# A hybrid decoder layer: moving activations at a stride of 1088 bytes, and row tiles that take turns in the down projection

## The chip, the cores and the metric

The kernel runs on one core of one Trainium2 chip. The metric is the device time of one execution in microseconds (us); the median of three runs stands for a kernel. The engines are named as in the profile: PE is TensorE (PEld its weight loads), DVE is VectorE, ACT is ScalarE, POOL is GpSimd, SP issues most of the DMAs.

## The reference

One decoder layer over 272 tokens (16 meta tokens and 256 of the sequence), model dimension 2048, all in float32:

```
u = rmsnorm(h);  proj = u @ w_in                       # 2048 x 7176
8 retention heads and 4 mLSTM heads -> mix (2048 features)
h = h + mix @ w_out                                    # 2048 x 2048, the output projection
u = rmsnorm(h);  up = causal_dwconv(u @ w_up)          # 2048 x 11264, the up projection
gate, val = split(up);  h = h + (silu(gate) * val) @ w_down   # 5632 x 2048, the down projection
return rmsnorm(h)[:, 16:]
```

## The kernel before

**Matrix products.** A weight is read once from HBM in pieces of 512 KB (`load_w`, lines 123 to 132), and split into two parts: ScalarE rounds it to float32r (`whi`, line 129) and VectorE takes the rest (`wlo`, line 131). The activations are split in the same way (`xh`/`xl`, `mixh`/`mixl`, `uh`/`ul`, `mh`/`ml`). A product is three matmuls per pair of tiles: high by high, high weight by low activation, low weight by high activation.

**Input, output and up projections** keep the activations feature-major: a tile `[128, 16, columns]` holds 16 feature tiles in a row of each partition. The weight (128 x 128) is the stationary operand, and one feature tile of the activations, all tokens, is the moving one. A piece of 512 KB is a half output tile: 8 feature tiles, so 24 matmuls (`mmk`, lines 134 to 141: eight pairs of lines 138 and 139, then eight of line 141). The moving columns are 272 tokens (`T`) in the input projections, or 258 (`NQ`, tokens 14 on) or 262 where the earliest tokens are not needed. `xh` and `xl` (lines 180 and 181) have 272 columns, so one feature tile lies 1088 bytes behind the last; a 258-column matmul on them reads from column 14. `mixh` and `mixl` (lines 175 and 176, 32 half tiles of the output projection at line 526) and `uh` and `ul` (lines 499 and 500, 176 half tiles of the up projection at line 595) have 258 columns, a stride of 1032 bytes.

**The down projection** (lines 587 to 648) turns the operands round. It runs twice, for each half of the 5632 features, after the up projection of that half. The weights are the moving operand, 512 columns; the stationary one is 128 tokens of `mh` or `ml`. A half has 4 blocks of 512 output columns (loop over `b`), a block has 11 steps (`q`), and a step has one 512 KB piece with two feature tiles. For each step `product` is called for row tile 0 (tokens 0 to 127), six matmuls into one PSUM bank, and then for row tile 1, six into another. In the last block of all row tile 1 runs 4 steps behind, so that row tile 0 is normed and stored meanwhile. `done` (line 620) adds a finished block to the residual; `finish` (line 571) does the last norm and the store.

**Order.** A scheduler of the framework orders the instructions by estimated times. All 512 KB pieces go through one DMA queue (SP) into 4 buffers (`wraw`); there are 5 buffers of `whi` and 5 of `wlo`. Output tiles of the projections rotate through 4 PSUM banks (`mmps`), blocks of the down projection through 4 others (`atps`). In the opening tiles (lines 195 to 226) the first head's k (`atps`) and q (`mmps`) and the gates run beside one another as the inputs arrive.

**The first norm** (lines 236 to 241) calls `rsqrt_m2`, whose two small tiles `r0` and `rt` come from the pool that is handed to it.

Of the kernel before, what the change touches and what calls it, by code (L numbers as in the profile page):

```python
# [10 lines left out]
F32 = mybir.dt.float32  # L11
F32R = mybir.dt.float32r
AF = mybir.ActivationFunctionType
ALU = mybir.AluOpType
# [10 lines left out]
TQ = T0 - 4  # first token of the mLSTM queries ahead of their convolution  # L25
# [7 lines left out]
GW = 64  # columns of the gates: i from 0, f from GW / 2  # L33
# [3 lines left out]
# Column ranges of the three blocks of (source, target) pairs: sources 0..127,  # L37
# 128..255 and 256..271 against the targets that can see them.
# [4 lines left out]
# Columns of the packed per-partition parameters.  # L43
# [9 lines left out]
NPAR0 = _COLS["gffn"][0]  # the columns before are for the heads  # L53
# [30 lines left out]
def trunk(ctx: ExitStack, tc: tile.TileContext, io, out: bass.AP):  # L84
# [35 lines left out]
    # ---- weights: a half of an output tile at a time, split in two float32r parts --  # L120
# [13 lines left out]
    def mmk(ps, w, ks, xh, xl, first, last):  # L134
        """Sum over ks, pairs of a k tile in w and one in the activations; first and last of these begin and end it."""
# [12 lines left out]
    def project(src, xh, xl, t0):  # L148
        """An output tile (128 features by tokens t0..) of a product over the model dim."""
        ps = mm.tile([P, 512], F32, name="mmps")  # L150
        for half in range(2):
            half_tile(ps[:, : xh.shape[2] - t0], src, half, xh, xl, t0)
        return ps

    def table(name, after):
        """Load a table of activations once the instruction before it has gone."""
# [3 lines left out]
    def rsqrt_m2(work, v, n, after):  # L160
        """-2 / sqrt(v + EPS), v in PSUM: a table's estimate and a Newton step."""
# [10 lines left out]
    # ================= input projections and the two kinds of heads ==================  # L172
    mixp_cm = pool("mixp", 1, side="left")
    mixp = mixp_cm.__enter__()
    mixh = mixp.tile([P, KT, NQ], F32R, name="mixh")
    mixl = mixp.tile([P, KT, NQ], F32R, name="mixl")
# [12 lines left out]
    # matmuls of nothing wake the tensor engine's clock while the first inputs come  # L189
# [4 lines left out]
    # the first tiles (gates, first head's k and q) run along the inputs as these arrive  # L194
    gates_ps, k_ps = (at.tile([P, 512], F32, name="atps") for _ in range(2))
    q_ps = mm.tile([P, 512], F32, name="mmps")
    with pool("sq", 3, side="right") as sqp:
        acc = None
        for k0, k1 in [(0, 1), (1, 2)] + [(k, k + 2) for k in range(2, KT, 2)]:
# [10 lines left out]
            # the gates' two parts lie side by side  # L210
# [16 lines left out]
            # mean square of the inputs  # L227
# [8 lines left out]
        with tc.high_priority():  # L236
# [3 lines left out]
            r = rsqrt_m2(sqp, ms[:, :T], T, copied)  # L240
            nc.vector.tensor_scalar(out=rstd1, in0=r, scalar1=-0.5, scalar2=None, op0=ALU.mult)
# [7 lines left out]
    # the output gate's sigmoid is (1 + tanh(x / 2)) / 2  # L249
# [4 lines left out]
    row = lambda name: pa.tile([MH, T], F32, name=name)  # noqa: E731  # L254
# [17 lines left out]
    # M and m in two parts, to be handed to all partitions  # L272
# [17 lines left out]
    def scaled(ps, t0, name, **kw):  # L290
        """A projection with its tokens' 1/rms."""
# [4 lines left out]
    def values(vts):  # L296
        """Token-major values, less their mean over the head, from feature-major ones."""
# [21 lines left out]
    def scores(kT, qT):  # L319
        """Transposed scores of the three blocks; qT starts at token T0."""  # L320
# [6 lines left out]
    def weigh(lhs, pT):  # L327
        """Sum over the sources of lhs(block) times the weights."""
# [6 lines left out]
    def variance(s2, mean):  # L335
        """Mean square over the head's features, on every partition."""
# [28 lines left out]
    def ret_project(h):  # L365
# [11 lines left out]
        # the last head's gate is left to run beside its attention  # L377
# [19 lines left out]
    def conv_silu(ps, f, t0, name):  # L397
        """From token t0: 0, or TQ for tokens T0.. alone."""
# [189 lines left out]
    for half in range(2):  # L588
# [43 lines left out]
        for b in range(4):  # L632
# [5 lines left out]
            for q in range(NQD + lag):  # L638
                if q < NQD:
                    ws[q] = load_w(io["wd"][b, half * NQD + q], [P, 2, 512], more if last and q % 2 else wpool)  # L640
                    product(pss[0], 0, q, ws[q])
                    if q == NQD - 1:
                        done(pss[0], 0, b)
                        if last:
                            finish(0)
# [87 lines left out]
```

## Time and profile before

| | |
|---|---|
| median of three runs | 1261.52 us (1261.25 to 1262.94) |
| span of the profiled execution, first to last instruction | 1259.1 us |
| mean granted TensorE clock over the span | 0.994 |
| TensorE busy | 1239.8 us, 98% of the span |
| weight loads (PEld) | 1180.7 us, 94% |
| VectorE, ScalarE, GpSimd busy | 820.4, 655.5, 84.3 us |
| moved by DMA | 224.11 MB, mean 178 GB/s |

No time of the profiled execution outside its span is given; the median of the runs is 2.4 us above the span. Busy time of TensorE is summed over instructions that overlap in a pipeline, so it says that the engine always had a matmul under way, and not how fast these followed one another. That is read from the starts in the timeline.

### The profile page before, as it was taken

To read this page: it belongs to the slowest core of one execution; us is meant where nothing else is said; L and a number is where in the kernel's file an instruction comes from. 1 tells how busy PE (TensorE), PEld (TensorE's weight loads), DVE (VectorE), ACT (ScalarE), POOL (GpSimd) and SP (SyncE) were. 2 spreads that over 40 slices of the span, in tenths; PEclk is the share of its full clock that TensorE was granted. 3 is DMA by queue.
4 is the path that set the end of the run, shared out by engine and by line. 5 is a ranking of instruction groups with operands and counts; after the bars stand their busy time and mean duration, and the time that the engine had idled before them with its cause. 6 is when DMAs were issued, how large, how long until landed. Compare 5 with 4: busy or idle time off the path is not lost.

```text
span 1259.1 us, 22241 instructions
## 1 busy us (share of the span) xinstructions
PE 1239.8 (98%) x9094; PEld 1180.7 (94%) x9094; DVE 820.4 (65%) x1184; ACT 655.5 (52%) x882; POOL 84.3 (7%) x83
## 2 busy tenths in 40 slices
PE   6999999999999999999999999999999999999996
PEld 6999999999999999999999998888999999998885
DVE  8866767766666666667776764445676776765452
ACT  5647565655556555655555553334555555554442
POOL 6100001111110111000000000000000000000010
PEclk8999999999999999999999999999999999999999
DMA  6764545555554556555556556555555655655661
GB/s 185 260 198 139 163 159 158 158 168 171 173 160 151 181 179 213 165 184 185 184 178 187 178 181 191 192 184 186 183 184 184 185 184 185 180 177 183 193 204 68
DMA packets 63591, 224.11 MB, mean 178 GB/s; under 512 B 7388, under 2 KB 8284, under 8 KB 63360
## 3 DMA queue, kind: packets, MB, share of 16 engines
q1 hardware_dynamic: 62832, 219.92, 55.4%
q0 software_dynamic: 656, 2.76, 0.7%
q8 instruction: 71, 1.16, 0.4%
q14 instruction: 32, 0.26, 0.1%
HBM read 220.56 MB, written 2.10 MB: 177 GB/s over the span
## 4 chain that ended last, share of the span: by engine, by line
PE 97%; issue 1%; DVE 1%; DMA 0%; ACT 0%; SPq 0%; ACTq 0%; DVEq 0%
PE mmps L138 25%; PE mmps L141 24%; PE mmps L139 24%; PE atps L615 7%; PE atps L618 7%; PE atps L614 6%; PE atps L330 1%; PE atps L322 0%; PE atps L307 0%; PE atps L332 0%; PE atps L331 0%; DMA hT<-in_xT 0%; PE atps L554 0%; DVE xl L208 0%; DVE whi L215 0%
## 5 line engine op out<-in xcount | busy, mean ns | idle before, releaser
L129 ACT CAST whi<-wraw 128x1024 fp32r<-128x1024 f32 x404 | 423.4, 1049 | 484.6 <-PE mmps L139 253.0
L131 DVE TENSOR_TENSOR wlo<-wraw,whi 128x1024 fp32r<-128x1024 f32 x404 | 495.4, 1227 | 202.5 <-ACT whi L129 195.1
L139 PE MATMUL mmps<-ul,whi 128*128 128x258 f32 x1408 | 345.9, 283 | 0.0
L138 PE MATMUL mmps<-uh,whi 128*128 128x258 f32 x1408 | 345.8, 282 | 0.0
L138 PEld LDWEIGHTS mmps<-uh,whi 128*128 128x128 f32 x1408 | 266.1, 189 | 0.1
L139 PEld LDWEIGHTS mmps<-ul,whi 128*128 128x128 f32 x1408 | 265.2, 188 | 0.1
L138 PE MATMUL mmps<-xh,whi 128*128 128x272 f32 (+2 forms) x880 | 224.6, 289 | 0.0
L139 PE MATMUL mmps<-xl,whi 128*128 128x272 f32 (+2 forms) x880 | 222.4, 286 | 0.0
L141 PE MATMUL mmps<-uh,wlo 128*128 128x258 f32 x1408 | 199.2, 284 | 0.0
L141 PEld LDWEIGHTS mmps<-uh,wlo 128*128 128x128 f32 x1408 | 182.5, 189 | 0.0
L138 PEld LDWEIGHTS mmps<-xh,whi 128*128 128x128 f32 x880 | 166.0, 189 | 1.2
L139 PEld LDWEIGHTS mmps<-xl,whi 128*128 128x128 f32 x880 | 166.2, 189 | 0.1
L615 PE MATMUL atps<-whi,ml 128*128 128x512 f32 x352 | 140.0, 398 | 0.0
L614 PE MATMUL atps<-whi,mh 128*128 128x512 f32 x352 | 138.0, 392 | 0.0
L141 PE MATMUL mmps<-xh,wlo 128*128 128x272 f32 (+2 forms) x880 | 129.6, 286 | 0.0
L141 PEld LDWEIGHTS mmps<-xh,wlo 128*128 128x128 f32 x880 | 117.1, 189 | 0.0
L559 DVE TENSOR_TENSOR cu<-mmps,rstd 128x258 f32<-128x258 f32 x88 | 37.6, 427 | 115.9 <-PE mmps L141 115.9
L618 PE MATMUL atps<-wlo,mh 128*128 128x512 f32 x352 | 110.5, 395 | 0.0
L615 PEld LDWEIGHTS atps<-whi,ml 128*128 128x128 f32 x352 | 66.1, 188 | 17.0
L618 PEld LDWEIGHTS atps<-wlo,mh 128*128 128x128 f32 x352 | 66.1, 188 | 16.1
L614 PEld LDWEIGHTS atps<-whi,mh 128*128 128x128 f32 x352 | 66.1, 188 | 14.9
L139 PE MATMUL mmps<-mixl,whi 128*128 128x258 f32 x256 | 63.2, 283 | 0.0
(203 smaller groups left out, 1051.3 us busy)
## 6 DMA issues: line engine op xcount, KB each, us to landing
wraw<-in_wu SPq DMA_DIRECT2D x176, 512.0 KB, 3.5
wraw<-in_wi SPq DMA_DIRECT2D x108, 512.0 KB, 3.6
wraw<-in_wd SPq DMA_DIRECT2D x88, 512.0 KB, 3.5
wraw<-in_wo SPq DMA_DIRECT2D x32, 512.0 KB, 3.6
wraw<-in_w SPq DMA_DIRECT2D x7, 320.0 KB, 4.3
out<-hn SPq DMA_DIRECT2D x8, 256.0 KB, 3.0
hT<-in_xT SPq DMA_DIRECT2D x7, 272.0 KB, 5.5
e<-in_decay POOLq DMA_DIRECT2D x8, 209.0 KB, 3.4
```

The costliest lines, as they stand in the source:

```text
L129: nc.scalar.copy(hi, raw)
L131: nc.vector.tensor_tensor(out=lo, in0=raw, in1=hi.bitcast(F32), op=ALU.subtract)
L138: nc.tensor.matmul(ps, hi[:, k, :], xh(kk), start=kk == first, stop=False)
L139: nc.tensor.matmul(ps, hi[:, k, :], xl(kk), start=False, stop=False)
L141: nc.tensor.matmul(ps, lo[:, k, :], xh(kk), start=False, stop=kk == last)
L330: nc.tensor.matmul(ps[:, 0:NQ], lhs(0, P), pT[:, 0:CA], start=True, stop=False)
L559: nc.vector.tensor_tensor(out=u, in0=ps[:, :NQ], in1=rstd2, op=ALU.mult)
L614: nc.tensor.matmul(ps, mh[:, k, rows], hi[:, i, :], start=k == 0, stop=False)
L615: nc.tensor.matmul(ps, ml[:, k, rows], hi[:, i, :], start=False, stop=False)
L618: nc.tensor.matmul(ps, mh[:, k, rows], lo[:, i, :], start=False, stop=k == NHF - 1)
```

## The change

The four activation tiles of the output and up projections get 14 columns more that nobody reads (`NS` = 272), so that one feature tile lies 1088 bytes behind the last. `product` takes the row tiles it is to serve, and in all blocks but the last alternates between the two at each matmul. The two tiles of the first norm's `rsqrt_m2` come from the pool `wk`, which stays open through the heads, and no longer from `sqp`, which closes here. Comments are dropped as well; these lines are left out.

```diff
+NS = NQ + 14
...
-    mixh = mixp.tile([P, KT, NQ], F32R, name="mixh")
-    mixl = mixp.tile([P, KT, NQ], F32R, name="mixl")
+    mixh = mixp.tile([P, KT, NS], F32R, name="mixh")[:, :, :NQ]
+    mixl = mixp.tile([P, KT, NS], F32R, name="mixl")[:, :, :NQ]
...
-            r = rsqrt_m2(sqp, ms[:, :T], T, copied)
-            nc.vector.tensor_scalar(out=rstd1, in0=r, scalar1=-0.5, scalar2=None, op0=ALU.mult)
+            r = rsqrt_m2(wk, ms[:, :T], T, copied)
+            nc.vector.tensor_scalar(out=rstd1, in0=r[:, :T], scalar1=-0.5, scalar2=None, op0=ALU.mult)
...
-    uh = up.tile([P, KT, NQ], F32R, name="uh")
-    ul = up.tile([P, KT, NQ], F32R, name="ul")
+    uh = up.tile([P, KT, NS], F32R, name="uh")[:, :, :NQ]
+    ul = up.tile([P, KT, NS], F32R, name="ul")[:, :, :NQ]
...
-        def product(ps, tt, q, w):
+        def product(outs, q, w):
             hi, lo = w
-            rows = slice(tt * P, (tt + 1) * P)
             for i in range(2):
                 k = 2 * q + i
-                nc.tensor.matmul(ps, mh[:, k, rows], hi[:, i, :], start=k == 0, stop=False)
-                nc.tensor.matmul(ps, ml[:, k, rows], hi[:, i, :], start=False, stop=False)
+                for m, first, last in ((mh, k == 0, False), (ml, False, False)):
+                    for tt, ps in outs.items():
+                        nc.tensor.matmul(ps, m[:, k, tt * P : (tt + 1) * P], hi[:, i, :], start=first, stop=last)
             for i in range(2):
                 k = 2 * q + i
-                nc.tensor.matmul(ps, mh[:, k, rows], lo[:, i, :], start=False, stop=k == NHF - 1)
+                for tt, ps in outs.items():
+                    nc.tensor.matmul(ps, mh[:, k, tt * P : (tt + 1) * P], lo[:, i, :], start=False, stop=k == NHF - 1)
...
             for q in range(NQD + lag):
+                outs = {}
                 if q < NQD:
                     ws[q] = load_w(io["wd"][b, half * NQD + q], [P, 2, 512], more if last and q % 2 else wpool)
-                    product(pss[0], 0, q, ws[q])
-                    if q == NQD - 1:
-                        done(pss[0], 0, b)
-                        if last:
-                            finish(0)
-                if q >= lag:
-                    product(pss[1], 1, q - lag, ws.pop(q - lag))
+                    outs[0] = pss[0]
+                if not lag:
+                    outs[1] = pss[1]
+                if outs:
+                    product(outs, q, ws[q])
+                if q == NQD - 1:
+                    done(pss[0], 0, b)
+                    if last:
+                        finish(0)
+                if lag and q >= lag:
+                    product({1: pss[1]}, q - lag, ws.pop(q - lag))
```

TensorE's queue, the first step of the down projection. `atps_8906` is the PSUM bank of row tile 0 and `atps_8907` that of row tile 1; behind the arrow stand the moving weights and the stationary activations. Before:

```order
L614 MATMUL atps_8906<-whi_8910,mh_5809 128x512
L615 MATMUL atps_8906<-whi_8910,ml_5810 128x512
L614 MATMUL atps_8906<-whi_8910,mh_5809 128x512
L615 MATMUL atps_8906<-whi_8910,ml_5810 128x512
L618 MATMUL atps_8906<-wlo_8912,mh_5809 128x512 x2
L614 MATMUL atps_8907<-whi_8910,mh_5809 128x512
L615 MATMUL atps_8907<-whi_8910,ml_5810 128x512
L614 MATMUL atps_8907<-whi_8910,mh_5809 128x512
L615 MATMUL atps_8907<-whi_8910,ml_5810 128x512
L618 MATMUL atps_8907<-wlo_8912,mh_5809 128x512 x2
```

Now:

```order
L617 MATMUL atps_8906<-whi_8910,mh_5809 128x512
L617 MATMUL atps_8907<-whi_8910,mh_5809 128x512
L617 MATMUL atps_8906<-whi_8910,ml_5810 128x512
L617 MATMUL atps_8907<-whi_8910,ml_5810 128x512
L617 MATMUL atps_8906<-whi_8910,mh_5809 128x512
L617 MATMUL atps_8907<-whi_8910,mh_5809 128x512
L617 MATMUL atps_8906<-whi_8910,ml_5810 128x512
L617 MATMUL atps_8907<-whi_8910,ml_5810 128x512
L621 MATMUL atps_8906<-wlo_8912,mh_5809 128x512
L621 MATMUL atps_8907<-wlo_8912,mh_5809 128x512
L621 MATMUL atps_8906<-wlo_8912,mh_5809 128x512
L621 MATMUL atps_8907<-wlo_8912,mh_5809 128x512
```

The same twelve matmuls stand in a step; the bank now changes at each of them, and the low weights come at the ninth place, where they came at the fifth. This repeats in 77 steps.

VectorE's queue, around the third block of the second half. `wlo` is the split of a weight piece, `hn<-atps,hn` the addition of a finished row tile. Before:

```order
L131 TENSOR_TENSOR wlo<-wraw,whi 128x1024 x14
L622 TENSOR_TENSOR hn<-atps,hn 128x512
L131 TENSOR_TENSOR wlo<-wraw,whi 128x1024
L622 TENSOR_TENSOR hn<-atps,hn 128x512
L131 TENSOR_TENSOR wlo<-wraw,whi 128x1024 x3
```

Now:

```order
L132 TENSOR_TENSOR wlo<-wraw,whi 128x1024 x15
L625 TENSOR_TENSOR hn<-atps,hn 128x512 x2
L132 TENSOR_TENSOR wlo<-wraw,whi 128x1024 x3
```

The first row tile's addition has moved behind one weight split; the other blocks' additions stand as before.

## Rows read from the trace of the kernel before

**Rows 1.** Page, busy time; then a window in the up projection.

```profile
PE 1239.8 (98%) x9094; PEld 1180.7 (94%) x9094; DVE 820.4 (65%) x1184; ACT 655.5 (52%) x882; POOL 84.3 (7%) x83
...
core 0: us, PE busy (x) PEld busy (x) DVE busy (x) ACT busy (x) POOL busy (x), PEclk, DMA share, GB/s
520.00:740.00 220.00, 220.00 (x1832) 220.00 (x1831) 152.78 (x226) 116.35 (x155) 0.00 (x0) 1.00 0.58 180
```

**Rows 2.** Waits of TensorE: us in total, times, longest us.

```profile
PE atps L141 <- DVE wlo L214: 7.4, 5, 2.0
```

**Rows 3.** Page, costliest groups: the weights' cast.

```profile
L129 ACT CAST whi<-wraw 128x1024 fp32r<-128x1024 f32 x404 | 423.4, 1049 | 484.6 <-PE mmps L139 253.0
```

**Rows 4.** Timeline of TensorE, up projection: start us, us, instruction.

```profile
555.65 0.28 PE L138 MATMUL mmps<-uh,whi 128*128 128x258 f32 x1
...
624.93 0.28 PE L138 MATMUL mmps<-uh,whi 128*128 128x258 f32 x1
```

**Rows 5.** Timeline of TensorE, output projection.

```profile
421.88 0.28 PE L138 MATMUL mmps<-mixh,whi 128*128 128x258 f32 x1
...
488.15 0.28 PE L138 MATMUL mmps<-mixh,whi 128*128 128x258 f32 x1
```

**Rows 6.** Timeline of TensorE, input projections, 272 columns.

```profile
74.03 0.29 PE L141 MATMUL mmps<-xh,wlo 128*128 128x272 f32 x1
...
83.05 0.29 PE L141 MATMUL mmps<-xh,wlo 128*128 128x272 f32 x1
```

**Rows 7.** Timeline of TensorE, input projections, 258 columns, stride 1088 bytes.

```profile
47.79 0.28 PE L138 MATMUL mmps<-xh,whi 128*128 128x258 f32 x1
...
53.57 0.28 PE L138 MATMUL mmps<-xh,whi 128*128 128x258 f32 x1
...
56.44 0.28 PE L138 MATMUL mmps<-xh,whi 128*128 128x258 f32 x1
...
59.29 0.29 PE L138 MATMUL mmps<-xh,whi 128*128 128x272 f32 x1
```

**Rows 8.** Timeline of TensorE, down projection.

```profile
789.66 0.39 PE L614 MATMUL atps<-whi,mh 128*128 128x512 f32 x1
...
796.66 0.39 PE L614 MATMUL atps<-whi,mh 128*128 128x512 f32 x1
```

**Rows 9.** Page, costliest groups: one line of the up and of the output projection.

```profile
L139 PE MATMUL mmps<-ul,whi 128*128 128x258 f32 x1408 | 345.9, 283 | 0.0
...
L139 PE MATMUL mmps<-mixl,whi 128*128 128x258 f32 x256 | 63.2, 283 | 0.0
```

**Rows 10.** Timeline of TensorE, one half tile of 258 columns, stride 1088.

```profile
269.91 0.28 PE L138 MATMUL mmps<-xh,whi 128*128 128x258 f32 x1
...
272.82 0.28 PE L342 MATMUL atps<-vh,inv_ret 128*128 128x258 f32 x1
```

**Rows 11.** Timeline of TensorE, opening tiles; then a tile of 262 columns.

```profile
6.66 0.29 PE L138 MATMUL atps<-xh,whi 128*128 128x272 f32 x1
6.79 0.28 PE L138 MATMUL mmps<-xh,whi 128*128 128x262 f32 x1
...
7.40 0.29 PE L223 MATMUL atps<-xh,whi 128*128 128x272 f32 x1
...
66.16 0.28 PE L138 MATMUL mmps<-xh,whi 128*128 128x262 f32 x1
...
72.02 0.29 PE L138 MATMUL mmps<-xh,whi 128*128 128x272 f32 x1
```

**Rows 12.** Timeline, last matmul and what follows.

```profile
1248.99 0.63 PE L618 MATMUL atps<-wlo,mh 128*128 128x512 f32 x2
...
1249.66 0.69 DVE L622 TENSOR_TENSOR hn<-atps,hn 128x512 f32<-128x512 f32 x1 [2.90 <-PE atps L618]
```

**Rows 13.** Timeline of VectorE, line 168: the first two uses.

```profile
49.00 0.44 DVE L168 SCALAR_TENSOR_TENSOR rt<-atps,rt 128x272 f32<-128x272 f32 x1
...
125.06 0.43 DVE L168 SCALAR_TENSOR_TENSOR rt<-atps,rt 128x258 f32<-128x258 f32 x1 [0.96 <-ACT rt L167]
```

## The prediction

> **What bounds the kernel now.** I read the busy times first, then who waits, then the pace of the matmuls. TensorE is busy for 98% of the span and the granted clock is 1.00 in the up projection, the 2.4 GHz level [rows 1]. The longest entry in TensorE's own list of waits is 7.4 us, for the low weights of the opening tiles (line 214, five times) [rows 2]. The weights are far ahead: ScalarE idles 484.6 us in front of its casts, 253.0 of them until TensorE frees a buffer [rows 3]. So no transfer, cast or copy is late once the program has started. The time is the number of matmuls multiplied by the distance from one start to the next, and a change to the order or the addresses can only count through that distance.
>
> The "mean ns" of a matmul group is a latency of overlapping instructions, not this distance. I take it from starts in the timeline, over stretches whose matmuls I can count (24 to a half output tile):
>
> - Up projection, 258 columns, stride 1032 bytes: 24 half tiles lie between 555.65 and 624.93 us [rows 4], so 69.28 us / 576 = **120.28 ns**.
> - Output projection, 258 columns, stride 1032: 23 half tiles in 66.27 us [rows 5], / 552 = **120.06 ns**.
> - Input projections, 272 columns, stride 1088, read from the row's start: 3 half tiles in 9.02 us [rows 6], / 72 = **125.28 ns**.
> - Input projections, 258 columns, stride 1088, read from column 14, which is 56 bytes into the row: 4 half tiles in 11.50 us, / 96 = **119.79 ns** [rows 7].
> - Down projection, 512 columns: 5 half steps of six in 7.00 us, / 30 = **233.3 ns** [rows 8].
>
> At 2.4 GHz and a column per cycle, 258, 272 and 512 columns are 107.5, 113.3 and 213.3 ns. So each matmul costs 12 to 20 ns beyond that, and that surplus is all that this change can touch.
>
> **The change part by part.**
>
> *Stride, up projection.* Three lines (138, 139, 141) of 1408 matmuls each, 4224 in all [rows 9]. Nothing is added to any engine: the tile is longer, the columns read stay 258. What changes is the start: k × 1032 bytes leaves every second feature tile 8 bytes past a multiple of 16, k × 1088 never does. The trace has no 258-column matmul at stride 1088 from the row's start, so I bound it by neighbours. Best: the 272-column pace less 14 columns at the 0.450 ns per column that lies between the 272 and the 512 pace ((233.3 − 125.28) / 240), 118.98 ns, a gain of 1.30 ns × 4224 = 5.5 us. Worst: the slowest half tile of 258 columns that I found at stride 1088, from 269.91 to 272.82 us [rows 10], 2.91 us / 24 = 121.25 ns, a loss of 0.97 × 4224 = 4.1 us. In between stand the two nearest rows: the 272 pace less 14 columns at 2.4 GHz (5.83 ns), 119.45 ns, which has the right start but other columns; and 119.79 ns, which has the right columns but another start. I take their middle, **119.6 ns**: a gain of 0.68 × 4224 = **2.9 us**.
>
> *Stride, output projection.* 768 matmuls (three lines of 256 [rows 9]), the same bounds: 0.46 ns × 768 = **0.35 us** gained, between 0.8 gained and 0.9 lost.
>
> *Row tiles in turn.* In seven of the eight blocks, 11 steps of 12 matmuls, 924 in all, every matmul now adds into the other PSUM bank than the one before, and the moving weights stay for four matmuls where they stayed for two. Count, columns and weight loads are the same. The nearest row is in the opening tiles: from 6.66 to 7.40 us six matmuls alternate between two banks, three of 272 and three of 262 columns, at 0.74 / 6 = 123.3 ns [rows 11]. Matmuls that stay in one bank take 125.28 ns (272) and (72.02 − 66.16) us / 48 = 122.1 ns (262) [rows 6, 11], mean 123.7. So turns alone give nothing: **0 us**. The rounding of two starts (10 ns over six) bounds it at 1.7 ns × 924 = 1.6 us either way; the far bound of a gain is the whole surplus, 20 ns × 924 = 18.5 us.
>
> *What waits on the new order.* The high weights of a step are now free after 8 of 12 matmuls, not 10, and the low ones are first needed at the ninth, not the fifth: both slacken. VectorE's addition of the first row tile (0.69 us [rows 12]) moves behind one weight split; before, it could start a half step earlier, 1.4 us. Nobody on the path waits for it, because the next block uses the other two banks. If that cover went (banks not free), a block would start up to 0.69 us late, 7 × 0.69 = 4.8 us. The last block keeps its lag, so the tail from the last matmul at 1248.99 us to the end of the span is untouched [rows 12]. ScalarE's, GpSimd's and the DMA queues' instructions stand in the same order as before.
>
> *The first norm's two buffers* come from another pool: used at 49.00 us, wanted again only by the first head's variance at 125.06 us [rows 13]. 0 us; if the two met, one VectorE instruction of 0.43 us would wait.
>
> **Sum:** 2.9 + 0.35 + 0 + 0 = 3.2 us off. The profiled execution's span is 1259.1 us; the median of the runs is 1261.52, 2.4 more, which I keep as what lies around a span. 1261.5 − 3.2 = **1258.3 us**.
>
> The Trainium skill ("SBUF — State Buffer", Specifications (TRN2)) gives cachelines of 16 bytes and a penalty at each crossing into a new line. By that rule 258 float32 touch 65 lines from either start, and the stride would give 0 us instead of 3.2. The rows cannot decide it: 120.28 ns for mixed starts against 119.79 ns for starts that are all 8 bytes off is a difference that neither the start nor the stride explains alone.
>
> **The rivals.**
>
> *No change.* The pace goes by columns and clock alone; 119.79 against 120.06 and 120.28 ns is the jitter of the pace, as neighbouring half tiles of one tile show (2.87 and 2.85 us, from 53.57 and 56.44 us [rows 7], against 2.91 us [rows 10]). The up projection stays near 120.2 ns: **1261.5 us**. [...]
>
> *Slower: the pace settles in its slow pattern.* The distance depends on addresses in a repeating way. All bases and strides move, and the up projection may repeat the 2.91 us of [rows 10]: 4.1 + 0.9 us = 5.0 lost, **1266.5 us**. It decides once the mean half tile of the up projection is over 2.90 us (2.5 us / 176 above today's 2.886). Against it: that half tile stands alone among tiles of attention, while four in a row ran at 11.50 us.
>
> *Turns pay too.* If part of the 20.0 ns surplus of a down matmul comes from following itself in a bank, and it fell to the 11.9 ns of the 272-column rows, 8.1 × 924 = 7.4 us more come off: **1250.9 us**. It counts from 2.7 ns a matmul on. Against it: the alternating rows [rows 11].
>
> **How the numbers follow.** Forecast 42%, no change 38%, slow pattern 10%, turns 10%. A measurement of this kernel can tell 0.2%, 2.5 us, from no change. The forecast lies only 0.7 us beyond that, so I give 36 of its 42 points to faster; with the turns and 2 points of the second case, faster is 0.48. Same gets the other 6 and 35 of no change: 0.41. Slower is the slow pattern and 1 point: 0.11. The range from 1252 to 1264.5 takes in the best bound of the stride (1261.5 − 6.3 = 1255.2), no change, and the near parts of the two outer cases; under 2 in 10 lies outside. The forecast's own range is 1255 to 1260.
>
> **What would show it.** Right: the up projection's half tiles at about 2.87 us instead of 2.886, 272-column ones unchanged at 3.007, the down matmuls still at 233 ns, TensorE still without waits. Wrong: an up pace of 120.2 ns or more (no change, or the slow pattern), or a down pace under 230.6 ns (turns). A new wait of TensorE at a block's start would be the additions.

## The result, and the profile after

The change made the kernel slower: **1264.31 us** (median of 20 runs, 1263.2 to 1265.88) against 1262.33 us for the kernel before (20 runs beside it), a ratio of 1.0016 [1.0009, 1.0022]. That is 2.0 us lost, where 3.2 us saved had been forecast. The profiled execution took 1263.85 us, its span 1262.1 us.

Page of the changed kernel, busy time; it answers to the first of [rows 1]:

```profile
PE 1243.3 (99%) x9094; PEld 1185.8 (94%) x9094; DVE 819.6 (65%) x1184; ACT 654.6 (52%) x882; POOL 86.9 (7%) x83
```

The same window in the up projection as in [rows 1] (us, each engine's busy time and instructions, PEclk, DMA share, GB/s):

```profile
520.00:740.00 220.00, 220.00 (x1824) 220.00 (x1823) 150.78 (x223) 115.67 (x154) 0.00 (x0) 1.00 0.59 180
```

TensorE is as full as before and the granted clock is 1.00 in both windows, but 1824 matmuls fit where 1832 did. So the matmuls are farther apart, and nothing waits. The longest entries of TensorE's waits (us in total, times, longest us) answer to [rows 2]. The second shown does not stand in the list of the kernel before. Of the short waits of the opening tiles, two of 0.8 and 0.5 us have given place to one of 0.5 us:

```profile
PE atps L142 <- DVE wlo L215: 7.1, 5, 2.4
...
PE atps L285 <- issue: 0.6, 1, 0.6
```

ScalarE's casts are as far ahead as in [rows 3] (idle 487.1 us, it was 484.6):

```profile
L130 ACT CAST whi<-wraw 128x1024 fp32r<-128x1024 f32 x404 | 423.3, 1048 | 487.1 <-PE mmps L140 255.5
```

The timeline of TensorE gives the paces (start us, us, instruction). The pairs are, in this order: input projections of 272 columns, 72 matmuls apart; output projection, 24 half tiles (576 matmuls); up projection, 78 half tiles (1872); down projection, 20 steps (240). Last come the final matmul and the addition that waits for it:

```profile
72.91 0.29 PE L139 MATMUL mmps<-xh,whi 128*128 128x272 f32 x1
...
81.93 0.29 PE L139 MATMUL mmps<-xh,whi 128*128 128x272 f32 x1
...
422.84 0.28 PE L139 MATMUL mmps<-mixh,whi 128*128 128x258 f32 x1
...
492.60 0.28 PE L139 MATMUL mmps<-uh,whi 128*128 128x258 f32 x1
...
522.63 0.28 PE L139 MATMUL mmps<-uh,whi 128*128 128x258 f32 x1
...
748.84 0.28 PE L139 MATMUL mmps<-uh,whi 128*128 128x258 f32 x1
...
779.63 0.39 PE L617 MATMUL atps<-whi,mh 128*128 128x512 f32 x1
...
835.40 0.39 PE L617 MATMUL atps<-whi,mh 128*128 128x512 f32 x1
...
1251.96 0.63 PE L621 MATMUL atps<-wlo,mh 128*128 128x512 f32 x2
...
1252.63 0.69 DVE L625 TENSOR_TENSOR hn<-atps,hn 128x512 f32<-128x512 f32 x1 [2.92 <-PE atps L621]
```

| distance between matmuls, ns | before, same stretches | after | difference x matmuls |
|---|---|---|---|
| input projections, 272 columns [rows 6] | 125.28 | 9.02 us / 72 = 125.3 | 0 |
| output projection [rows 5] | 120.07 | 69.76 us / 576 = 121.11 | 1.04 x 768 = +0.8 us |
| up projection [rows 4] | 120.28 | 226.21 us / 1872 = 120.84 | 0.56 x 4224 = +2.4 us |
| down projection [rows 8] | 233.3 | 55.77 us / 240 = 232.4 | -0.9 x 1056 = -1.0 us |

The sum is +2.2 us, against 2.0 measured. The spans differ by 3.0 us. The rest lies ahead of the output projection, whose counted stretch starts at 422.84 us where it started at 421.88: in the experiments below that leave the input projections and the weights' buffers alone, that start lies anywhere from 421.98 us (`m8u4`) to 423.94 us (`s1056`), so the rest is within the scatter of the opening.

So there are two things to explain: why the stride made the 258-column matmuls slower, and why the down projection became faster.

### The profile page after: what moved, and what is told of

It is laid out like the page before. It is cut to its first block, busy times and chain, and to the rows that moved or that the text cites. A ratio compares the mean times of both kernels' runs of the same rounds, so it can differ in the third digit from the quotient of the medians.

```text
span 1262.1 us, 22241 instructions
## 1 busy us (share of the span) xinstructions
PE 1243.3 (99%) x9094; PEld 1185.8 (94%) x9094; DVE 819.6 (65%) x1184; ACT 654.6 (52%) x882; POOL 86.9 (7%) x83
## 4 chain that ended last, share of the span: by engine, by line
PE 97%; issue 1%; DVE 1%; DMA 0%; ACT 0%; SPq 0%; ACTq 0%; DVEq 0%
PE mmps L139 25%; PE mmps L140 24%; PE mmps L142 24%; PE atps L617 13%; PE atps L621 6%; PE atps L331 1%; DMA hT<-in_xT 0%; PE atps L323 0%; PE atps L308 0%; PE atps L333 0%; PE atps L332 0%; PE atps L555 0%; PE atps L324 0%; DVE whi L216 0%; ACT xh L208 0%
## 5 line engine op out<-in xcount | busy, mean ns | idle before, releaser
L130 ACT CAST whi<-wraw 128x1024 fp32r<-128x1024 f32 x404 | 423.3, 1048 | 487.1 <-PE mmps L140 255.5
L617 PE MATMUL atps<-whi,ml 128*128 128x512 f32 x352 | 113.9, 395 | 0.0
L617 PE MATMUL atps<-whi,mh 128*128 128x512 f32 x352 | 113.9, 395 | 0.0
L621 PE MATMUL atps<-wlo,mh 128*128 128x512 f32 x352 | 97.9, 395 | 0.0
L628 POOL TENSOR_TENSOR hn<-hn,gfin 128x512 f32<-128x512 f32 x8 | 14.1, 1778 | 746.4 <-ACT junk L627 746.4
```

The costliest lines, as they stand in the source:

```text
L130: nc.scalar.copy(hi, raw)
L617: nc.tensor.matmul(ps, m[:, k, tt * P : (tt + 1) * P], hi[:, i, :], start=first, stop=last)
L621: nc.tensor.matmul(ps, mh[:, k, tt * P : (tt + 1) * P], lo[:, i, :], start=False, stop=k == NHF - 1)
L628: nc.gpsimd.tensor_tensor(out=h, in0=h, in1=gfin[:, b * 512 : (b + 1) * 512], op=ALU.mult)
```

## The experiments

All paces below are read in the timeline as above: up over 78 half tiles of the first half, output over 24, down over 20 steps, unless a line says otherwise. The expectations give means over all distances of a stage, which lie up to 0.4 ns from these stretches, and in two kernels farther, of which more below. Single runs scatter by some 1 us; where the mechanism is in question the paces decide, not the times. A pace is the mean of a repeating pattern and not the distance of every pair: in the up projection of the changed kernel the distances run from 113 to 125 ns in a cycle of 24 matmuls, and each half tile from the 13th to the 87th of the first half takes 2.900 us.

"Starting byte" is the first byte that a matmul reads of a feature tile, modulo 64, as the program allocates it. `mixh`, `mixl`, `uh` and `ul` begin on a multiple of 64 and `xh` and `xl` 32 bytes past one. In the kernel before the sixteen feature tiles step through 0, 8, 16 ... 56; in the change all of them start at 0.

### Each part alone

The first kernel has the edits of the four activation tiles and of the norm's buffers, the second has the new `product` and the new loop, as in the diff above. (`s_only`, five rounds:)

> The kernel before with the stride of 1088 bytes alone (and the first norm's buffers from the other pool); the down projection as before. Theory A (the pace of a matmul follows a repeating pattern that the addresses of its operands set, and the new addresses have a slower one): up projection 120.8 ns from start to start, output projection 121.0, down projection 233.3; 4224 x 0.5 + 768 x 0.9 = 2.9 us slower, ratio 1.0023. Rival, the change's parts do not add (what the trace of the change shows in the up projection comes from the turns or from a state of that run): up projection back at 120.3, ratio within 0.9995 to 1.0005.

(`t_only`, five rounds:)

> The kernel before with the row tiles taking turns alone; all strides as before. Theory A: up and output projections at 120.3 and 120.1 ns as before, down projection 232.4 ns; 924 x 0.9 = 0.8 us faster, ratio 0.9993. Rival (turns do nothing by themselves, 232.4 is the run's): down projection 233.3 ns, ratio 1.000.

Up (1872 matmuls apart) and down projection (240 apart) of `s_only`, then of `t_only`:

```profile
523.37 0.28 PE L139 MATMUL mmps<-uh,whi 128*128 128x258 f32 x1
...
749.57 0.28 PE L139 MATMUL mmps<-uh,whi 128*128 128x258 f32 x1
...
769.21 0.39 PE L615 MATMUL atps<-whi,mh 128*128 128x512 f32 x1
...
824.98 0.39 PE L615 MATMUL atps<-whi,mh 128*128 128x512 f32 x1
```

```profile
521.21 0.28 PE L138 MATMUL mmps<-uh,whi 128*128 128x258 f32 x1
...
746.37 0.28 PE L138 MATMUL mmps<-uh,whi 128*128 128x258 f32 x1
...
766.06 0.39 PE L615 MATMUL atps<-whi,mh 128*128 128x512 f32 x1
...
822.06 0.39 PE L615 MATMUL atps<-whi,mh 128*128 128x512 f32 x1
```

The stride alone: 1264.63 us, ratio 1.0023 [1.0014, 1.0032]. Its paces are those of the change: up 120.83, output 121.11, **and down 232.4 ns**, without the turns, where 233.3 had been expected. The turns alone: 1262.42 us, ratio 1.0002 [0.9993, 1.0011]; up 120.28, output 120.07, down 233.3 ns, as before, which is the rival's number. So the turns do nothing, and the whole result, the faster down projection included, comes with the stride. (The norm's buffers are in the first kernel too and have no run of their own; the kernels further down that differ from it only in the column read leave them as they are.)

### A start elsewhere, and another stride

The change, its four tiles read from column 14 of the 272 (starting byte 56; one of the four lines is shown); then the change with 264 and with 260 columns (strides of 1056 and 1040 bytes, so the starts step through 0 and 32, or through 0, 16, 32, 48).

```diff
-    uh = up.tile([P, KT, NS], F32R, name="uh")[:, :, :NQ]
+    uh = up.tile([P, KT, NS], F32R, name="uh")[:, :, 14 : 14 + NQ]
```

> The change, with the four tiles read from column 14 of their 272, as the input projections read theirs: every feature tile then starts 56 bytes into its 1088-byte row. Theory A: the pattern moves with the addresses, pace of the up projection anywhere from 119.2 to 121.2 ns. Rival B (starts that are all equally placed are what is slow, wherever they lie): 120.8 ns in the up projection, 121.0 in the output projection. The prediction's neighbour would give 119.8 ns.

> The change, with a stride of 1056 bytes (264 columns): starts still at multiples of 32 bytes, but eight feature tiles no longer at multiples of 64. Theory A: a pace of its own, from 119.2 to 121.2 ns, with a pattern that repeats in another way than at 1088. Rival C (starts on multiples of 16 bytes cost more than mixed ones, the opposite of the prediction): 120.8 ns again. Down projection 232.4 ns by both.

> The change, with a stride of 1040 bytes (260 columns): every feature tile starts on a multiple of 16 bytes, as with 1088, and steps through all such places. Theory A: 119.2 to 121.2 ns, a pattern of its own. Rival C: 120.8 ns in the up projection, 121.0 in the output projection. The prediction's reason (no start half way in 16 bytes) would give 119.6 ns.

Measured: 1260.6, 1262.8 and 1256.59 us (one run each). The stride of 1088 and the equal starts are the same in the first as in the change, and its output projection goes at 119.44 ns where the change's takes 121.11: rival B fell. The stride of 1056 gave up 120.42 and output 120.56 ns, 1040 gave 119.44 and 119.24. Multiples of 16 bytes are therefore not slow in themselves, and rival C fell. The stride of 1040 came where the prediction's reason puts it (119.6), but the same reason had put the change there. So the place where the tiles start counts, and not only whether it is a multiple of 16 bytes.

The first of them showed something else. Its up projection in the first half (the first pair, 1872 matmuls) and in the second (the second pair, 1824):

```profile
521.78 0.28 PE L139 MATMUL mmps<-uh,whi 128*128 128x258 f32 x1
...
748.50 0.28 PE L139 MATMUL mmps<-uh,whi 128*128 128x258 f32 x1
...
891.34 0.28 PE L139 MATMUL mmps<-uh,whi 128*128 128x258 f32 x1
...
1109.20 0.28 PE L139 MATMUL mmps<-uh,whi 128*128 128x258 f32 x1
```

That is 121.11 and 119.44 ns: the same instructions on the same bytes keep one pace through one half and another through the other.

### The down projection's rhythm

The kernel before, with one matmul of 64, 32, 96 or 128 columns that nobody reads ahead of blocks 0 and 2 of each half:

```diff
+            if q == 0 and tt == 0 and b in (0, 2):
+                n = {(0, 0): 64, (0, 2): 32, (1, 0): 96, (1, 2): 128}[half, b]
+                nothing = at.tile([P, 512], F32, name="atps")
+                nc.tensor.matmul(nothing[:, :n], mh[:, 0, 0:P], hi[:, 0, :n], start=True, stop=True)
```

> The kernel before with four matmuls of nothing (32 to 128 columns, into a bank that nobody reads) ahead of blocks 0 and 2 of each half of the down projection. Nothing else of the stage differs. Theory H (the stage has more than one steady rhythm and keeps the one into which it falls at its start; the change did not make the down projection faster, its entry did): at least one of the four stretches leaves the rhythm of two matmuls (229 and 238 ns, 233.3 mean) for the rhythm of seven (232.4 mean). Rival (the pace of the down projection is set by its addresses and order): 233.3 ns in all four stretches.

Its timeline in the first half, 252 matmuls between the 64-column and the 32-column extra, then 252 behind the 32-column one:

```profile
752.31 0.40 PE L618 MATMUL atps<-whi,mh 128*128 128x512 f32 x1
...
811.11 0.40 PE L618 MATMUL atps<-whi,mh 128*128 128x512 f32 x1
...
814.01 0.40 PE L618 MATMUL atps<-whi,mh 128*128 128x512 f32 x1
...
872.57 0.40 PE L618 MATMUL atps<-whi,mh 128*128 128x512 f32 x1
```

58.80 and 58.56 us: 233.3 ns, and 232.4 ns behind an extra of 32 columns, in a kernel that moves no byte of an operand. In the second half 252 matmuls behind the extra of 96 columns and 120 behind that of 128 go at 232.4 ns too, so theory H, which asked for one of the four stretches, has three. (An extra takes one of the four PSUM banks, so the blocks' pairs of banks change. That is not the cause: the pair of the first block behind the 32-column extra also serves the second and the fourth block of a half in the kernel before, at 233.3 ns.) So the stage has (at least) two steady paces and keeps the one it is pushed into. The whole kernel took 1262.44 us beside 1261.08, one run each, its extra matmuls included. A later kernel shows the same from the other side: `m14u10`, which has the new stride and the turns, ran its down projection at 233.3 ns (777.62 to 833.62 us for 240).

### Which operand's place

The change with a gap of 32 bytes ahead of the weight buffers (`wshift`): the weights, the output projection's tiles and `mh` and `ml` move by 32 bytes together, while `uh`, `ul`, `xh` and `xl` stay.

```diff
     consts = ctx.enter_context(pool("consts", 1, side="left"))
+    consts.tile([P, 8], F32, name="gap")
```

> The change, with 32 bytes of nothing ahead of the weights' buffers. That moves the weights by 32 bytes, the output projection's activations by the same 32 bytes, and leaves the up projection's activations where they are. Theory M (the moving operand's address alone sets the pattern): up projection 120.83 ns as in the change, output projection off its 120.99. Theory R (the place of the moving operand relative to the weights that are loaded beside it sets the pattern): up projection off its 120.83 by 0.2 ns or more, output projection 120.99 as in the change.

The change, with the output tiles read from column 8 (byte 32) and the up tiles from column 4 (byte 16), `m8u4`:

> The change, with the output projection's tiles read from column 8 (32 bytes into the row) and the up projection's from column 4 (16 bytes). Theory A (a pattern of its own for each place): each stage has a pace between 119.2 and 121.2 ns that differs from the change's by 0.2 or more. Rival C (starts on multiples of 16 bytes are slow): 121.0 and 120.8 ns again.

The up projection's stretch in the first, and below it in the second:

```profile
524.23 0.29 PE L140 MATMUL mmps<-uh,whi 128*128 128x258 f32 x1
...
749.39 0.29 PE L140 MATMUL mmps<-uh,whi 128*128 128x258 f32 x1
```

```profile
520.71 0.28 PE L139 MATMUL mmps<-uh,whi 128*128 128x258 f32 x1
...
741.18 0.28 PE L139 MATMUL mmps<-uh,whi 128*128 128x258 f32 x1
```

With the gap up goes at 120.28 ns although its tiles did not move, and the output stays at 121.11 although its tiles did (1263.75 us). The input projections, whose activations did not move either, slow down as well: the mean of the 272-column distances rises from 125.13 to 125.72 ns, that of the 258-column ones from 120.17 to 120.45. With the tiles at byte 16 the up projection goes at **117.77 ns**, 3.1 under the change, and the kernel at 1249.66 us. This looked as if the distance between the moving tile and the weights decided (theory R). Three kernels were to test it: the weights' data 16 bytes further in and everything else in its place modulo 64 (`w16`; its weight buffers are 64 bytes longer, so they also lie 4160 bytes apart and no longer 4096), all four tiles at byte 16 without the turns (`m4u4`), and output and up at bytes 8 and 48 (`m2u12`).

```diff
-        hi = to.tile(shape, F32R, name="whi", bufs=n)
+        def room(name):
+            return to.tile([P, 1040], F32R, name=name, bufs=n)[:, 4 : 4 + 1024].rearrange("p (a b) -> p a b", a=shape[1])
+
+        hi = room("whi")
...
-        lo = to.tile(shape, F32R, name="wlo", bufs=n)
+        lo = room("wlo")
```

> The change, with the data of each weight buffer begun 16 bytes further in (16 of 64); the activation tiles stand where the change has them, byte for byte modulo 64. Theory R (the place of the moving operand relative to the weights loaded beside it sets the pace; 16 of 32 bytes apart is the good place): the up projection falls from 120.83 to about 117.8 ns a matmul and the output projection from 120.99 to 117.8, though their moving tiles have not moved; together 4224 x 3.0 + 768 x 3.2 = 15 us, so some 1249 us. If the rule holds for the other products too, the 272 column ones (125.1 ns, 32 bytes apart) and the down projection (232.5 ns, 0 apart: its weights move, its stationary is the middle) fall as well and the time goes under 1249. Rival A (the moving operand's own start modulo 32 sets the pace): up and output stay at 120.8 and 121.0, only the down projection, whose moving weights now start at 16, falls.

> The kernel before with the stride of 1088 bytes and all four activation tiles read from column 4 (16 bytes in), without the turns. Theory R and rival A alike: up 117.8 ns as in the run m8u4, and now the output projection also 117.8 ns (it was 120.44 at 32 bytes): 768 x 2.64 = 2.0 us under m8u4's 1249.7, so about 1247.6 us. If the output stays at 120 ns, the good place is not a matter of the bytes alone. The down projection between 232.4 and 233.3 ns, whichever rhythm it falls into (0.9 us).

> The change with the output projection's tiles read from column 2 (8 bytes in) and the up projection's from column 12 (48 bytes in). If 16 of 32 bytes is the good place, up goes at 117.8 ns as at 16 bytes; if 16 of 64 alone is good, it lies near 120. The output at 8 bytes: near 120.1 ns, the pace of the kernel before, whose k tiles step through all multiples of 8. Time about 1250 us in the first case, 1261 in the second.

The up projection of `w16`, and of `m4u4`:

```profile
522.30 0.28 PE L142 MATMUL mmps<-uh,whi 128*128 128x258 f32 x1
...
749.93 0.28 PE L142 MATMUL mmps<-uh,whi 128*128 128x258 f32 x1
```

```profile
520.19 0.28 PE L139 MATMUL mmps<-uh,whi 128*128 128x258 f32 x1
...
740.67 0.28 PE L139 MATMUL mmps<-uh,whi 128*128 128x258 f32 x1
```

Moving the weights made it worse: 121.6 ns in up and output, 1267.38 us, ratio 1.0041 [1.0026, 1.0056]; the down projection stayed at 232.3 ns, the mean of the 272-column distances rose from 125.12 to 125.46, and that of the input projections' 258-column ones fell from 120.17 to 119.80. **Theory R fell**: 16 bytes apart is good when the activations move and bad when the weights do. So did rival A, because the pace moved while the activations stood still. A difference with a sign (weights at 16 and activations at 0 as 48 of 64) does not save the theory: with the weights at 0, activations at byte 48 go at 118.9 to 120.3 ns in the table below and not at 121.6, and with the gap up should then have gone as at byte 32, at 119.86, and went at 120.28. Both places count, and their difference alone does not give the pace. (The Trainium skill, "TensorE: Matmul & The Clock Gate", Step-by-step: what each phase is for, has the moving operand and the weight loads on two read ports of their own, so that loading weights takes no bandwidth from a running matmul. Moving the weights alone changed the pace here, from 120.83 to 120.28 and to 121.6 ns, so their place counts too. The recorded weight loads of the up projection take a mean of 188 to 191 ns in all these kernels. Whether the two reads meet after all, or the pace changes in another way, the runs do not show.) In `m4u4` the paces held: up 117.78, output 117.94 ns, **1249.33 us, ratio 0.9899 [0.9883, 0.9916]**. The time is 1.7 us above the 1247.6 expected: the output projection takes 1.8 us less than in `m8u4`, but begins 1.3 us later, behind an opening and input projections that both kernels share. It is the best kernel of the study. `m2u12` took 1257.8 us; its output at byte 8 went at 120.00 ns, as expected, and its up projection at byte 48 at 120.28 ns in the first half and 118.89 in the second, a second case of two paces on the same bytes. Neither is the 117.8 ns of byte 16, so "16 of 32 bytes" is not the rule.

### The eight places

The change with only the columns altered at which the tiles are read (columns 2 to 12 of 272), to fill the map:

> The change with the output tiles read from column 6 (24 bytes in) and the up tiles from column 2 (8 bytes in). Theory P (the pace of a matmul belongs to its starting byte, and a changing start pays the mean): the four known places of up are 120.83 (0), 117.80 (16), 119.56 (48), 120.23 (56); for the mean of all eight to be the 120.30 of the kernel before, the four missing ones must average (8 x 120.30 - 478.42) / 4 = 121.0, and since the strides of 1040 and 1056 bytes (119.47 and 120.41) put byte 32 at 119.7 to 120.0, bytes 8, 24 and 40 must average 121.4. So up here near 121.4 by P. Theory N (a rhythm not tied to bytes): no sum holds. Rival D (8 byte offsets cost nothing of their own): near 120.0, as the output at 8 bytes (119.97).

> The change with the output tiles from column 10 (40 bytes) and the up tiles from column 8 (32 bytes). Theory P: up at 119.7 to 120.0 ns, the value that the strides of 1040 and 1056 bytes leave for byte 32 (4 x 119.47 - 120.83 - 117.80 - 119.56 = 119.7, 2 x 120.41 - 120.83 = 120.0); by N anything between 117.8 and 121.6. The output at 40 bytes is a new place.

> The change with the output tiles from column 12 (48 bytes) and the up tiles from column 6 (24 bytes). Theory P: up near 121.4 ns, with bytes 8 and 40 averaging that with it. The output at 48 bytes by the stride of 1040 bytes: 4 x 119.30 - 120.99 - 118.15 - 120.44 = 117.6 ns.

> The change with the output tiles from column 14 (56 bytes, as in the run col14: 119.52 ns) and the up tiles from column 10 (40 bytes). Theory P: up is what is left for the mean of the eight places to be 120.30 ns, about 121.4; the output repeats 119.52 within 0.1 ns. By N the output need not repeat.

The up projection's stretch (78 half tiles) at bytes 8, 32, 24 and 40, one fence for each kernel:

```profile
522.40 0.28 PE L139 MATMUL mmps<-uh,whi 128*128 128x258 f32 x1
...
747.04 0.28 PE L139 MATMUL mmps<-uh,whi 128*128 128x258 f32 x1
```

```profile
523.25 0.28 PE L139 MATMUL mmps<-uh,whi 128*128 128x258 f32 x1
...
747.63 0.28 PE L139 MATMUL mmps<-uh,whi 128*128 128x258 f32 x1
```

```profile
521.14 0.28 PE L139 MATMUL mmps<-uh,whi 128*128 128x258 f32 x1
...
743.79 0.28 PE L139 MATMUL mmps<-uh,whi 128*128 128x258 f32 x1
```

```profile
521.92 0.28 PE L139 MATMUL mmps<-uh,whi 128*128 128x258 f32 x1
...
746.73 0.28 PE L139 MATMUL mmps<-uh,whi 128*128 128x258 f32 x1
```

| starting byte | 0 | 8 | 16 | 24 | 32 | 40 | 48 | 56 | mean |
|---|---|---|---|---|---|---|---|---|---|
| up, ns | 120.83 | 120.00 | 117.78 | 118.94 | 119.86 | 120.09 | 120.28, 118.89 | 121.11, 119.44 | 119.7 |
| output, ns | 121.11 | 120.00 | 117.94 | 120.28 | 120.28 | 120.86 | 119.12 | 119.44 | 119.9 |

(Two numbers are the two halves, and count with their mean. The output's 117.94 at byte 16 has two slower half tiles at its start; the other 22 go at 117.8 ns, as up does.) The times were 1260.27, 1260.55, 1254.73 and 1261.06 us, one run each. Theory P expected the four missing places of the up projection to average 121.0, so that the mean of all would be the 120.3 of the kernel before. They average 119.72, and byte 32 alone came where it was expected; byte 8 came where rival D had it (120.0), and the output at byte 48, expected at 117.6, went at 119.12. So the old stride did not pay the mean of the eight places: it paid 0.6 ns more in the up projection and 0.2 in the output. The output at byte 56 repeated its 119.44 in a second kernel. Nor does a place give every half tile the same time: at byte 32, where all matmuls start alike, the half tiles of up alternate between 119.6 and 120.1 ns a matmul.

### Is it the byte or the rhythm

The change with one small matmul of nothing ahead of four tiles of each half of the up projection; then the change with 274 columns (a stride of 1096 bytes, which steps through the eight places as 1032 does); then `m4u4` with the head projections' tiles `xh`, `xl` moved too, the 258-column reads from byte 24 to 16 and the 272-column ones from 32 to 24.

```diff
+                if s == 0 and jj in (2, 8, 14, 20):
+                    n = {2: 32, 8: 64, 14: 96, 20: 200}[jj]
+                    nothing = at.tile([P, 512], F32, name="atps")
+                    nc.tensor.matmul(nothing[:, :n], uh[:, 0, 0:P], uh[:, 1, :n], start=True, stop=True)
```

> The change with one matmul of nothing (32, 64, 96 or 200 columns, its output read by nobody) ahead of the tiles 2, 8, 14 and 20 of each half of the up projection: eight disturbances of the rhythm, none of a byte. If the pace belongs to the starting byte (theory P), up stays at 120.83 ns after each of them, and the half tile at 2.900 us. If it is a rhythm that the stage falls into (theory N), as in the down projection, some stretch between two disturbances settles at another pace, by tenths of a nanosecond or more.

> The change with a stride of 1096 bytes instead of 1088: again steps of 8 bytes modulo 64, so that the sixteen k tiles start at all eight places, as with 1032 bytes. If the old pace belongs to stepping through the places, up is 120.3 and the output 120.1 ns as in the kernel before, and the time is that of before (1261 to 1263 us). If the row of 1032 bytes had a cost of its own, up falls to the mean of the eight places, 119.67 ns, and the time to about 1259.5 us.

> The kernel m4u4 (stride 1088, output and up tiles 16 bytes in; 1249.3 us) with the head projections' tiles moved too: those of 272 columns from byte 32 to 24 of 64, and with them those of 258 columns from byte 24 to 16. If the up projection's map holds there, the 272 column matmuls fall by 119.87 - 118.96 = 0.9 ns from 125.12 to 124.2 (1274 counted), the 258 column ones by 118.96 - 117.80 = 1.2 ns from 120.17 to 119.0 (1147 counted): 1.2 + 1.3 = 2.5 us, so 1246.8 us. If the map belongs to the up projection and its weights' place alone, these move by up to 1 ns either way and the time stays within 1 us of 1249.3.

In the first, the 96-column extra of the first half, then 22 half tiles (528 matmuls) behind it, then 22 behind the 64-column extra of the second half:

```profile
658.83 0.21 PE L599 MATMUL atps<-uh 128*128 128x96 f32 x1
...
661.85 0.28 PE L139 MATMUL mmps<-uh,whi 128*128 128x258 f32 x1
...
725.65 0.28 PE L139 MATMUL mmps<-uh,whi 128*128 128x258 f32 x1
...
970.52 0.28 PE L139 MATMUL mmps<-uh,whi 128*128 128x258 f32 x1
...
1034.32 0.28 PE L139 MATMUL mmps<-uh,whi 128*128 128x258 f32 x1
```

63.80 us both times, 2.900 us a half tile (120.83 ns), and so behind every one of the eight extras (1264.46 us). At byte 0 the up projection came back to 120.83 ns from all eight pushes. With the weights where the change has them, bytes 0 and 16 never showed another pace there, in either half of any kernel; bytes 48 and 56 did. So some places were seen with one steady pace and some with two.

The stride of 1096 gave 1262.79 us beside 1262.12, with up at 120.9 and output at 119.59 ns: stepping by 8 bytes is not better than before, and again not the mean of the places.

The last gave 1249.84 us, ratio 0.9902 [0.9886, 0.9919], no gain over `m4u4`, where 2.5 us had been expected if the up projection's map held. Its 272-column matmuls, 72 apart:

```profile
74.56 0.29 PE L139 MATMUL mmps<-xh,whi 128*128 128x272 f32 x1
...
83.73 0.29 PE L139 MATMUL mmps<-xh,whi 128*128 128x272 f32 x1
```

They went from 125.3 to 127.4 ns, against the map, while the mean distance of the 258-column ones fell from 120.17 to 118.12 (1147 and 1145 of them). So byte 16 is the best place seen for 258 columns in three stages; the map does not carry over to 272.

## Why the prediction was wrong

**What bounds the kernel: right.** No transfer, cast or addition became late, the clock stayed at its upper level in the window read, and the result is the sum of matmul counts by distances.

**Stride, up projection: this step failed.** It took 119.6 ns from two neighbours and forecast 2.9 us saved; the change pays 120.83 ns and loses 2.4. The prediction described a start by whether it is a multiple of 16 bytes, and so took for neighbours reads that start at byte 32 (272 columns) and at byte 24 (column 14 of `xh`). Neither stands at byte 0, where the change puts every tile. The map shows 3 ns between byte 0 and byte 16, both multiples of 16. The mean over the eight places, 119.7 ns, lies beside the forecast of 119.6, but that does not bear out the reason: the four multiples of 16 bytes average 119.5 and the four places between them 119.8, a small step beside the 3 ns among the multiples themselves. The stride removes the stepping, and byte 0 costs more than the stepping did. The nearest row itself was thin as well: 119.79 ns came from 96 matmuls, and all 1147 of its kind in the changed kernel's trace average 120.17.

**Stride, output projection: the same failure**, 121.11 ns instead of a gain of 0.46: 0.8 us lost, at the end of the stated bound (0.9).

**Turns: right**, 0 us: alone they give a ratio of 1.0002 [0.9993, 1.0011]. The rival in which they pay fell.

**What waits on the new order, and the norm's buffers: right.** The last addition starts 0.67 us behind the last matmul's start, as in [rows 12], and no wait on a bank appeared.

**Not in the sum: the down projection.** It was to stay at 233 ns and gave back 1.0 us, and not through the turns. The extra matmuls show that it has two steady paces on the same bytes. Which one it enters by changes with what runs ahead of it; how, was not followed further.

**The rival "slow pattern" was right in kind.** It said that the up projection may repeat its slow half tile, and that this decides above 2.90 us; the half tiles now take 2.900, just at that mark. Whether it is the same pattern is not shown. It overpriced the loss: 5.0 us for both stages against 3.2, of which the down projection returned 1.0. The reason given against it, that the slow half tile stood alone, was no reason: the next stage has other starting bytes.

**The page's rule.** By the cachelines of 16 bytes ("SBUF — State Buffer" in the Trainium skill, Specifications (TRN2)) 258 float32 touch 65 lines from any of the eight places, so all would cost the same. The measured paces run from 117.8 to 121.1 ns. The rule alone does not give the pace here.

**What stays open** is the mechanism. Shown are: of the change's parts the stride is the cause; the place within 64 bytes of the activations, and that of the weights too, changes the pace; their difference alone does not give it; some places have two paces. Which port, buffer or queue makes it so was not tried, nor whether places 64 bytes and more apart differ. One rival was not tried by a run: that the reads and writes of the other engines slow the matmuls. The half tiles speak against it, all 2.900 us long while VectorE is busy for 150.78 us of the 220 us window and the DMA engines for a share of 0.59; but work that TensorE itself paces could repeat as evenly.

## What to carry to other kernels

A row stride that is a multiple of 64 bytes pins every feature tile to one starting byte, and in this kernel the choice of that byte weighs more than the stride: reading the padded tiles from column 4 instead of 0 took the padded kernel from 1264.6 to 1249.3 us with no instruction more. Where TensorE never waits, read the distance of starts over a long stretch, and try the start columns one by one; here a neighbour's pace carried over neither to another byte, nor to other columns, nor to another place of the weights. Float32r with 128 x 128 weights was the only form tried. A gain or loss of a few tenths of a per cent in a stage that an edit does not touch can be the stage's other steady rhythm.

## What the runs showed of the hardware that was not expected

- The distance of 258-column float32r matmuls with a weight load each depends on the starting byte of the moving tile: 117.8 ns at byte 16, 120.8 at 0 (up projection), 117.9 and 121.1 (output).
- Moving the weights under unmoved activations changes it as well: 120.83 to 120.28 ns with the weights at byte 32 (`wshift`), to 121.6 at 16 (`w16`, buffers 4160 bytes apart).
- A stage can hold two steady paces on identical bytes: 121.11 and 119.44 ns at byte 56, 120.28 and 118.89 at byte 48, 233.3 and 232.4 in the down projection, where one 32-column matmul switched it.
